# Row sums of a 32x512x1024 array on one core: one leading load of 128 consecutive rows, or two

## The chip, the cores and the metric

The kernel runs on one core of a Trainium2 chip. The metric is the device time of one execution in microseconds (us): the median of 3 runs before the change is 160.50 us (160.48 to 160.57).

## What is computed

```
x = randn(32, 512, 1024) as float32, multiplier = 0.5
out = (sum of x over its last axis * multiplier) as float32      # 32 x 512
```

That is 16,384 rows of 1024 numbers, 67.11 MB to be read, and one number per row, 0.07 MB, to be written.

## The kernel before, in words

The array is seen as 16,384 rows of 4 KB, and the 128 partitions take 128 rows each. The rows are cut in three parts:

- **The head** (L112): the first 128 rows, one row for each partition, in one load of 512 KB. ACT sums and scales each row (`act_row`, L90) into one column of the tile `column`, which DVE has cleared (L113). DVE then transposes `column` into `row` in blocks of 32x32 (L117), so that the 128 results lie in four partitions, 32 in each, and leave in a store of four runs (L188).
- **The middle** (L123 to L154): partition p takes 111 consecutive rows, so the partitions stand 111 rows apart in memory. They come in seven blocks: one of 15 rows per partition and six of 16 (`sizes`, L43), in three buffers. DVE sums a block in one instruction (`reduce_sum`, L136) into `sums` and scales it into `res` (L142). Only in the seventh block are eight of the 16 rows summed by ACT (L153).
- **The last block** (L156 to L212): 16 consecutive rows per partition, in pieces. p0 is ten rows, p1 four, p2 one row and 384 numbers of the next, e0 352 numbers, e1 the last 288. ACT and DVE share their rows; DVE uses `dve_sum` (L99), and its last instruction adds up the parts of row 15 (L210).

All loads and stores are issued by SP, in the order of the program text, into one hardware queue. A load waits on SP only if it needs a buffer that DVE frees (`free`, on `dve_done`) or is to come behind a landing (`behind`). The loads that wait for nothing, the head and the first three blocks, are moved to the program's entry by a hook (`start_loads_at_entry`, L223), ahead of SP's first drain, so that they start before the other engines do.

Around the change SP's order at the end is: loads p0, p1, p2, e0, e1 (L163 to L182); a wait for the seventh block's scaled sums (L183); the **early store** of the middle's results (L184), which waits for ACT too; the head's store (L188); and the **last store** of the last block's results (L214), which waits for the last sums. SP then waits for the early and the head's store, drains, and waits for the last one (L218 to L221).

Of the kernel before, what the change touches and what calls it, by code (L numbers as in the profile page):

```python
# [9 lines left out]
def kernel(  # L10
# [13 lines left out]
    nc = tc.nc  # L24
# [4 lines left out]
    P = nc.NUM_PARTITIONS  # L29
# [3 lines left out]
    x_flat = x.flatten_outer_dims()  # L33
    N, D = x_flat.shape
    rows = N // P
    out_flat = out.rearrange("b s -> (b s)")
    mul = float(multiplier)

    B = 16
    n_blocks = rows // B  # L40
    assert N == P * rows and rows == n_blocks * B
    Q = 32
    sizes = [B - 1] + [B] * (n_blocks - 2)  # L43
    own = 1 + sum(sizes)
    x_rows = x_flat[P : P * own, :].rearrange("(p c) d -> p c d", p=P)
    x_last = x_flat[P * own : N, :].rearrange("(p c) d -> p c d", p=P)
    out_head = out_flat[0:P].rearrange("(q c) -> q c", c=Q)
    out_rows = out_flat[P : P * own].rearrange("(p c) -> p c", p=P)
    out_last = out_flat[P * own : N].rearrange("(p c) -> p c", p=P)

    def sbuf(name, *shape):
        return ctx.enter_context(nc.sbuf_tensor(name, list(shape), fp32)).ap()
# [2 lines left out]
    buf = [sbuf(f"xb{i}", P, B, D) for i in range(bufs)]  # L55
    sums = sbuf("sums", P, rows)
    res = sbuf("res", P, rows)
    head = sbuf("head", P, 1, D)
    column = sbuf("column", P, Q)
    row = sbuf("row", P, Q)  # L60
    cuts = [384, 736, D]
# [3 lines left out]
    def sem(name):  # L65
        return nc.alloc_semaphore(name=name)
# [5 lines left out]
    def marks(i, engine):  # L72

        s = dve_done if engine == "dve" else act_done
        i.then_inc(s, 1)
        counts[engine] += 1
        return counts[engine]

    def load(name, dst, src, free=None, behind=None):

        landed = sem(name)
        i = nc.sync.dma_start(out=dst, in_=src)  # L82
        if free is not None:
            i.wait_op(dve_done, free, "sem-ge")
        if behind is not None:
            i.wait_op(behind, 16, "sem-ge")
        i.then_inc(landed, 16)
        return landed

    def act_row(t, r, dst):  # L90
        return nc.scalar.activation(  # L91
            out=t[:, r, :],
            in_=t[:, r, :],
            func=mybir.ActivationFunctionType.Copy,
            scale=mul,
            accum_out=dst,
        )
# [11 lines left out]
            accum_out=dst,  # L109
        )  # L110

    landed_head = load("landed_head", head[:, 0, :], x_flat[0:P, :])  # L112
    cleared = marks(nc.vector.memset(column, 0.0), "dve")  # L113
    nc.scalar.wait_ge(landed_head, 16)
    nc.scalar.wait_ge(dve_done, cleared)
    summed = marks(act_row(head, 0, column[:, 0:1]), "act")
    turned = nc.vector.transpose(out=row, in_=column)  # L117
    turned.wait_op(act_done, summed, "sem-ge")
    marks(turned, "dve")
# [1 line left out]
    freed = []  # L121
    blocks = []
    for b, n in enumerate(sizes):  # L123
        c0 = 1 + sum(sizes[:b])
        t = buf[b % bufs][:, 0:n, :]
        landed = load(
            f"landed{b}",
            t,
            x_rows[:, c0 - 1 : c0 - 1 + n, :],
            freed[b - bufs] if b >= bufs else None,  # L130
        )
        blocks.append(landed)
        h = n if b < n_blocks - 2 else n // 2
        nc.vector.wait_ge(landed, 16)
        done = marks(
            nc.vector.reduce_sum(  # L136
                out=sums[:, c0 : c0 + h], in_=t[:, 0:h, :], axis=mybir.AxisListType.X
            ),
            "dve",
        )  # L140
        freed.append(done)
        scaled = nc.vector.tensor_single_scalar(  # L142
            out=res[:, c0 : c0 + h],
            in_=sums[:, c0 : c0 + h],
            scalar=mul,
            op=mybir.AluOpType.mult,
        )
        scaled.wait_op(dve_done, done, "sem-ge")
        early_dve = marks(scaled, "dve")
        if h < n:  # L150
            nc.scalar.wait_ge(landed, 16)
            for r in range(h, n):
                i = act_row(t, r, res[:, c0 + r : c0 + r + 1])  # L153
            early_act = marks(i, "act")  # L154

    c0 = own  # L156
# [23 lines left out]
            )  # L180
        )
    ]  # L182
    nc.sync.wait_ge(dve_done, early_dve)  # L183
    early = nc.sync.dma_start(out=out_rows, in_=res[:, 1:own])  # L184
    early.wait_op(act_done, early_act, "sem-ge")
    early_stored = sem("early_stored")
    early.then_inc(early_stored, 16)
    first = nc.sync.dma_start(out=out_head, in_=row[0:P:Q, :])  # L188
    first_stored = sem("first_stored")
    first.then_inc(first_stored, 16)  # L190

    summed_up = sem("summed_up")
    on_act = {1, 4, 7, 9, 13, 14}
# [22 lines left out]
    stored = sem("stored")  # L216
    store.then_inc(stored, 16)
    nc.sync.wait_ge(early_stored, 16)  # L218
    nc.sync.wait_ge(first_stored, 16)
    nc.sync.drain()  # L220
    nc.sync.wait_ge(stored, 16)  # L221

# [62 lines left out]
```

## Time and profile before

| what | value |
|---|---|
| median of 3 runs | 160.50 us (160.48 to 160.57) |
| the profiled execution: its own time | 160.47 us |
| its span | 159.2 us |
| DVE busy | 119.1 us, 75% |
| ACT busy | 17.4 us, 11% |
| DMA packets | 2168, 67.18 MB, mean 422 GB/s over the span |
| chain that ended last | DMA 74%, DVE 24% |
| SP's longest wait behind the stores | 9.7 us, until DVE's last sum |

The span runs from the first recorded instruction, SP's issue of the head, to the end of the last store; the execution's own time is 1.27 us longer. The DMA row of the page's second part is the mean busy share of 16 DMA engines in tenths, and a packet is booked where it is recorded, so that a slice with few and the next with many packets belong together. L136 is a line of the kernel. In a timeline, each row gives the start and the duration in microseconds, the engine, the line, the operation, its tiles and shapes, and in brackets how long the engine had been idle and what ended that. What SP waited for gives, behind the colon, the microseconds in all, the number of waits and the longest.

### The profile page before, as it was taken

The page shows a single profiled execution, that of the slowest core. Times are in us where ns is not written, and L with a number is a line of the kernel's source. Part 1 is how long each engine was busy: PE and PEld are TensorE (multiplying, and loading weights), DVE is VectorE, ACT ScalarE, POOL GpSimd, SP SyncE. Part 2 cuts the span into 40 slices and gives each one's busy share as a digit, 9 for nine tenths or more (in the row PEclk, how much of TensorE's full clock was granted, in tenths as well). Part 3 has the DMA queues.
Part 4 walks back from the last instruction along what each step waited for, and adds up shares of the span by engine and source line. Part 5 has one row for each costly group of instructions (what it writes and reads, how often), then busy time and mean ns, then how long its engine had stood idle before and what let it go on. Part 6 is the DMA issues. An engine that isn't in the chain of part 4 may idle for free.

```text
span 159.2 us, 131 instructions
## 1 busy us (share of the span) xinstructions
DVE 119.1 (75%) x40; ACT 17.4 (11%) x31; POOL 0.2 (0%) x4
## 2 busy tenths in 40 slices
DVE  0000059995799968999599995999959999598376
ACT  2300000000000000000000000000000000397384
POOL 0000000000000000000000000000000000000000
DMA  9997996996997999969969969969989799798994
GB/s 379 494 401 340 494 527 264 527 527 264 527 461 329 527 395 395 527 280 511 527 264 527 527 264 527 494 296 527 445 346 527 346 445 527 329 453 371 420 401 151
DMA packets 2168, 67.18 MB, mean 422 GB/s; under 512 B 504, under 2 KB 760, under 8 KB 1016
## 3 DMA queue, kind: packets, MB, share of 16 engines
q1 hardware_dynamic: 2168, 67.18, 98.0%
HBM read 67.11 MB, written 0.07 MB: 422 GB/s over the span
## 4 chain that ended last, share of the span: by engine, by line
DMA 74%; DVE 24%; another core or an unknown queue 1%; SPq 1%; issue 0%
DMA xb<-in_x_dram 74%; DVE sums L136 22%; DVE xb L101 1%; SPq L82 1%; DVE end L101 0%; DVE res L142 0%; DVE res L101 0%
## 5 line engine op out<-in xcount | busy, mean ns | idle before, releaser
L136 DVE TENSOR_REDUCE sums<-xb 128x16 f32<-128x16384 f32 (+2 forms) x7 | 110.9, 15849 | 28.4 <-DMA xb<-in_x_dram 28.4
L91 ACT ACTIVATE xb<-xb 128x1024 f32<-128x1024 f32 x14 | 14.6, 1045 | 137.1 <-DMA xb<-in_x_dram 137.1
L101 DVE CUSTOM_DVE_ANT_0 xb<-xb 128x512 f32<-128x512 f32 (+1 forms) x10 | 5.9, 652 | 4.4 <-DMA xb<-in_x_dram 4.4
L91 ACT ACTIVATION_READ_ACCUMULATOR xb<-xb 128x1 f32 x14 | 2.6, 187 | 0.0
L113 DVE MEMSET column<- 128x32 f32 x1 | 0.1, 85 | 3.0 <-PEq L26 3.0
L117 DVE STREAM_TRANSPOSE row<-column 128x32 f32<-128x32 f32 x1 | 0.2, 212 | 2.6 <-ACT head L91 2.6
L91 ACT ACT_TABLE_LOAD x1 | 1.3, 1283 | 3.1 <-DVE column L113 3.1
L142 DVE TENSOR_SCALAR res<-sums 128x16 f32<-128x16 f32 (+2 forms) x7 | 1.2, 174 | 0.2
L91 ACT ACTIVATE head<-head 128x1024 f32<-128x1024 f32 x1 | 1.1, 1056 | 0.0
L101 DVE DVE_READ_ACCUMULATOR2_ANT res<- 128x1 f32 x10 | 0.8, 80 | 0.0
L101 DVE CUSTOM_DVE_ANT_0 end<-end 128x176 f32<-128x176 f32 (+1 forms) x2 | 0.7, 326 | 0.0
L91 ACT ACTIVATION_READ_ACCUMULATOR head<-head 128x1 f32 x1 | 0.2, 186 | 0.0
L101 DVE DVE_READ_ACCUMULATOR2_ANT end<- 128x1 f32 x2 | 0.2, 82 | 0.0
L266 POOL MEMSET const-bfloat16-1.0<- 128x1 bf16 x1 | 0.1, 101 | 0.0
L266 POOL MEMSET const-uint8-127<- 128x1 uint8 x1 | 0.1, 101 | 0.0
L266 POOL MEMSET const-float32-0.0<- 128x1 f32 x1 | 0.1, 98 | 0.2 <-issue 0.2
L266 POOL MEMSET const-float32-1.0<- 128x1 f32 x1 | 0.1, 98 | 0.0
## 6 DMA issues: line engine op xcount, KB each, us to landing
xb<-in_x_dram SPq DMA_DIRECT2D x1, 7680.0 KB, 21.2
xb<-in_x_dram SPq DMA_DIRECT2D x1, 5120.0 KB, 33.6
xb<-in_x_dram SPq DMA_DIRECT2D x1, 2048.0 KB, 36.4
xb<-in_x_dram SPq DMA_DIRECT2D x1, 704.0 KB, 20.8
head<-in_x_dram SPq DMA_DIRECT2D x1, 512.0 KB, 3.3
end<-in_x_dram SPq DMA_DIRECT2D x1, 176.0 KB, 19.2
end<-in_x_dram SPq DMA_DIRECT2D x1, 144.0 KB, 10.8
xb<-in_x_dram SPq DMA_DIRECT2D x6, 40.8
```

The lines of the kernel that those rows point to most:

```text
L82: i = nc.sync.dma_start(out=dst, in_=src)
L91: return nc.scalar.activation(out=t[:, r, :], in_=t[:, r, :], func=mybir.ActivationFunctionType.Copy, scale=mul, accum_out=dst,)
L101: return nc.vector.tensor_tensor_reduce(out=row[:, 0:mid], in0=row[:, 0:mid], in1=row[:, mid:], scale=scale, scalar=0.0, op0=ADD, op1=ADD, ...
L113: cleared = marks(nc.vector.memset(column, 0.0), "dve")
L117: turned = nc.vector.transpose(out=row, in_=column)
L136: nc.vector.reduce_sum(out=sums[:, c0 : c0 + h], in_=t[:, 0:h, :], axis=mybir.AxisListType.X),
L142: scaled = nc.vector.tensor_single_scalar(out=res[:, c0 : c0 + h], in_=sums[:, c0 : c0 + h], scalar=mul, op=mybir.AluOpType.mult,)
L266: nc = _bacc.Bacc("TRN2", target_bir_lowering=False, num_devices=1)
```

## The change

The head becomes two loads of 128 consecutive rows (`H = 2`), 512 KB each. Both are summed by ACT, into columns 0 and 1, and the transpose waits for the second. The middle has 110 rows per partition, in one block of 14 and six of 16. The last block is as before. The results of the two heads lie in partitions 0, 32, 64, 96 and 1, 33, 65, 97 of `row` and leave in two stores; these are now issued before the early store and before SP's wait for the scaled sums, right behind e1. The second head is one of the loads moved to the entry. Cut to what runs differently:

```diff
-    sizes = [B - 1] + [B] * (n_blocks - 2)
-    own = 1 + sum(sizes)
-    x_rows = x_flat[P : P * own, :].rearrange("(p c) d -> p c d", p=P)
+    H = 2
+    sizes = [B - H] + [B] * (n_blocks - 2)
+    own = H + sum(sizes)
+    x_rows = x_flat[P * H : P * own, :].rearrange("(p c) d -> p c d", p=P)
...
-    out_head = out_flat[0:P].rearrange("(q c) -> q c", c=Q)
-    out_rows = out_flat[P : P * own].rearrange("(p c) -> p c", p=P)
+    out_head = out_flat[0 : P * H].rearrange("(h q c) -> h q c", h=H, c=Q)
+    out_rows = out_flat[P * H : P * own].rearrange("(p c) -> p c", p=P)
...
-    head = sbuf("head", P, 1, D)
+    head = sbuf("head", P, H, D)
...
-    landed_head = load("landed_head", head[:, 0, :], x_flat[0:P, :])
+    landed_head = [
+        load(f"landed_h{h}", head[:, h, :], x_flat[h * P : (h + 1) * P, :]) for h in range(H)
+    ]
     cleared = marks(nc.vector.memset(column, 0.0), "dve")
-    nc.scalar.wait_ge(landed_head, 16)
     nc.scalar.wait_ge(dve_done, cleared)
-    summed = marks(act_row(head, 0, column[:, 0:1]), "act")
+    for h in range(H):
+        nc.scalar.wait_ge(landed_head[h], 16)
+        summed = act_row(head, h, column[:, h : h + 1])
+    summed = marks(summed, "act")
...
+    first_stored = sem("first_stored")
+    for h in range(H):
+        first = nc.sync.dma_start(out=out_head[h], in_=row[h:P:Q, :])
+        first.then_inc(first_stored, 16)
     nc.sync.wait_ge(dve_done, early_dve)
-    early = nc.sync.dma_start(out=out_rows, in_=res[:, 1:own])
+    early = nc.sync.dma_start(out=out_rows, in_=res[:, H:own])
     early.wait_op(act_done, early_act, "sem-ge")
     early_stored = sem("early_stored")
     early.then_inc(early_stored, 16)
-    first = nc.sync.dma_start(out=out_head, in_=row[0:P:Q, :])
-    first_stored = sem("first_stored")
-    first.then_inc(first_stored, 16)
...
-    nc.sync.wait_ge(first_stored, 16)
+    nc.sync.wait_ge(first_stored, 16 * H)
```

More of the change, by code (lines that the diff above doesn't have):

```diff
@@ L123 @@
     for b, n in enumerate(sizes):
-        c0 = 1 + sum(sizes[:b])
+        c0 = H + sum(sizes[:b])
         t = buf[b % bufs][:, 0:n, :]
@@ L128 @@
             t,
-            x_rows[:, c0 - 1 : c0 - 1 + n, :],
+            x_rows[:, c0 - H : c0 - H + n, :],
             freed[b - bufs] if b >= bufs else None,
```

## The prediction

> **What bounds the kernel now.** I read the chain that ended last first, then the slices and the queue, then the timeline for landing times, then what SP waited for. From the chain in order of time:
>
> ```profile
> 0.91 40.05 DMA xb<-in_x_dram
> ...
> 77.61 40.77 DMA xb<-in_x_dram
> 118.38 0.02 issue
> 118.39 36.35 DMA xb<-in_x_dram
> 154.75 0.02 issue
> 154.77 0.69 DVE xb L101
> ...
> 157.36 0.31 DVE end L101
> 157.67 0.01 DVE res L101
> ```
>
> Loads carry the chain, and its last DMA piece ends at 154.75 us. That is the landing of p1 (rows 10 to 13 of the last block, issued at 118.4). From there to 157.68 DVE works without a gap: the last two pieces, e0 and e1, are there when it reaches them. Then the last store is issued (0.34 us) and lands 1.4 us after its issue. The page's slices and queue say why the loads take that long:
>
> ```profile
> DMA  9997996996997999969969969969989799798994
> ...
> q1 hardware_dynamic: 2168, 67.18, 98.0%
> ```
>
> The 16 DMA engines work for 98.0% of the span; the digits of 6 and 7 stand beside slices of 527 GB/s and are packets booked where they end. In the timeline of DVE, each bracket shows that DVE waited for a load, so each start is a landing:
>
> ```profile
> 21.62 16.15 DVE L136 TENSOR_REDUCE sums<-xb 128x15 f32<-128x15360 f32 x1 [15.82 <-DMA xb<-in_x_dram]
> ...
> 40.98 17.22 DVE L136 TENSOR_REDUCE sums<-xb 128x16 f32<-128x16384 f32 x1 [3.00 <-DMA xb<-in_x_dram]
> ...
> 137.75 8.69 DVE L136 TENSOR_REDUCE sums<-xb 128x8 f32<-128x8192 f32 x1 [1.93 <-DMA xb<-in_x_dram]
> ...
> 149.88 0.69 DVE L101 CUSTOM_DVE_ANT_0 xb<-xb 128x512 f32<-128x512 f32 x1 [3.23 <-DMA xb<-in_x_dram]
> ...
> 154.77 0.69 DVE L101 CUSTOM_DVE_ANT_0 xb<-xb 128x512 f32<-128x512 f32 x1 [1.13 <-DMA xb<-in_x_dram]
> ```
>
> From 40.98 to 137.75 five blocks of 8,388,608 bytes land: 19.354 us each, 433.4 GB/s. From block 0 to block 1 it is 19.36 us, the same rate. So the queue never ran dry, from the first block on, and the end is the start of the stream, plus 67.11 MB at 433.4 GB/s, plus what each load adds, plus a tail of DVE and store. DVE is busy 75%, waits about 1.9 us for every block, and sets no landing.
>
> **The change, part by part.** The profiled execution took 160.47 us, of which 159.2 are the span, so 1.27 lie around it; I leave those 1.27 as they are. The median of the runs is 160.50, 0.03 above; I add that at the end.
>
> *One load more, of 128 rows.* The bytes stay: 512 KB move from block 0 (15 rows per partition, now 14) into a second head. Block 0 keeps its 128 packets (one for each partition), so 128 packets of 4 KB and 16 for the semaphore are added to the 2168, nine for each DMA engine. What does a load cost beyond its bytes? The landings of the last block tell, at 433.4 GB/s: p0, 5,242,880 bytes, should take 12.10 us and took 12.13 (149.88 - 137.75), 0.03 more. p1, 2,097,152 bytes, should take 4.84 and took 4.89, 0.05 more. p2, 720,896 bytes in packets of 5.5 KB, should take 1.66; ACT, idle until then, starts on it at 156.50, so it took 1.73, 0.07 more. The upper end is the head itself: it landed 3.3 us after its issue at 0, and block 0, 7,864,320 bytes or 18.15 us later, landed at 21.62, which leaves 0.17. The lower end: none of the five large blocks shows a cost apart from its rate, so 0 is possible. I take p2's **+0.07 us**, since its packets are nearest in size to 4 KB, and keep 0 and 0.17. It falls on the path in full: every later landing, p1's too, stands behind it in the stream.
>
> *The start.* The first load is the same one, issued at 0.00. Each load issue at the entry takes SP about 0.44 us (0.39 to 0.43 plus a gap of 0.05), so block 0's issue moves from 0.44 to about 0.88. Data flow from about 1.06 us (the first DMA slices show them there, 1.06 after the issue); the first head's 0.52 MB keep the engines until about 1.06 + 1.21 = 2.3 and the second's until 3.5, while block 0's first bytes can flow at 0.88 + 1.06 = 1.9. No gap: cost **0**. Without that cover it would be at most the 0.44 of one issue. Blocks 1 and 2 move by 0.44 too and are needed more than 15 us later.
>
> *SP gets to the entry barrier 0.44 us later.* DVE's memset now starts at 2.95 after it, so everything behind it moves: memset about 3.4, table load 3.55, first head activation 4.85.
>
> *The second head's sum.* ACT does one more ACTIVATE (1.06 us) and one more accumulator read (0.19); the transpose waits for both, at about 7.0 instead of 5.59, and takes 0.21 with two filled columns as with one. Both engines are idle there: DVE until 21.62, ACT until 137.75. Cost **0**, with 14 us of cover. The head's landing at about 4.5 is no later than ACT reaches it.
>
> *Block 0 of 14 rows.* Its sum shortens from 16.15 by one row, 17.22 - 16.15 = 1.07, and frees its buffer at about 36.8 instead of 37.8. Block 3's load is then issued 1 us sooner, into a queue that holds blocks 1 and 2, the latter landing at 60.4. No engine would have idled, so the gain is **0**.
>
> *The stores.* Now SP issues e1 (146.47), the early store (146.91, 0.37 us), and the result row (147.33, 0.64 us). After: e1 first as before, then two result rows at 0.64 each, then the early store at about 148.2 instead of 146.9. What follows on SP is the wait for the last store:
>
> ```profile
> SPq L214 <- DVE res L101: 9.7, 1, 9.7
> ```
>
> So 9.7 us become about 9.0 and the last store's issue at 157.70 doesn't move. In the queue, the early store landed 10.6 us after its issue, at 157.5, behind e1 (issued 146.47, 10.8 us to landing, 157.3): stores issued behind e1 wait behind e1, and issuing them 1.3 us later changes no order among loads. What is new is that on the few engines that serve a four-partition store there stand two packets of 128 B and their semaphore writes where one stood, before the early store's packets. By the pace of the early store (eight packets and one semaphore write per engine in about 0.2 us between 157.3 and 157.5) that is some 0.04 us, on a store that SP would not miss before the last one lands at 159.1: **0**, at worst 0.04. The early store's rows go from 444 to 440 bytes: no term.
>
> *The pitch of the rows.* Every block's partitions now stand 110 rows (440 KB) apart in HBM instead of 111 (444 KB). The trace has three pitches already: one row (the head), 111 rows (433.4 GB/s) and 16 rows, 64 KB (p0: 432.2 with its 0.03, p1: 428.9 with its 0.05). The 64 KB pitch, a pure power of two, loses nothing beyond the per-load cost, so for 440 KB, 55 times 8 KB, I take **0**. The bound above is p1's 428.9 for all that is loaded at this pitch (110 rows of 512 KB, 57.7 MB): 134.5 us against 133.1, +1.4. In the other direction nothing is to be had that a trace shows. The Trainium skill, in "DMA: Bandwidth & Descriptors", section "Latency and other measured facts", says that copies with per-partition row pitches at large powers of two lose rate and that padding the pitch by 4 KiB brings it back; by that rule an odd count of 4 KB rows is the safe pitch and this change gives it up. Against it stands p0 at a 64 KB pitch; no run here shows 440 KB.
>
> *Sum:* 160.47 + 0.07 = 160.54; on the median's scale **160.57 us**.
>
> **Rivals.** A measurement of this kernel can tell about 0.2%, 0.32 us, from no change; so "faster" is below 160.18 and "slower" above 160.82.
>
> *A, the forecast:* the extra load costs 0 to 0.17, 160.50 to 160.67. For it: four loads whose cost is read off, and a queue that is full throughout. Chance 0.64; within 0.2%.
>
> *B, the extra cost of a small first load is paid once:* the 0.17 between head and block 0 are then the time in which the engines change from the head to the first large block, and with 1 MB ahead it is hidden instead of doubled. 160.50 - 0.17 = 160.33. For it: that excess is the largest of the four. Against: block 0's first bytes could already flow at 0.44 + 1.06 = 1.5 us, 0.8 before the head's end. Chance 0.13; within 0.2%.
>
> *C, slower, the pitch:* a 440 KB pitch makes concurrent reads of the 16 engines collide in HBM. Its place is the seven blocks, its price 57.7 MB at the lower rate: each GB/s lost costs 133.1/433.4 = 0.31 us, so from about 1 GB/s on it decides. At p1's 428.9 it is 160.57 + 1.4 = 162.0; a middling loss of 2 GB/s gives 161.2. For it: the rows leave no spare rate, and the pitch gains a factor of two. Against: 64 KB does no harm. Chance 0.12.
>
> *D, the moved stores:* the two four-partition stores take more in the queue than a packet each and push the early store past the last one's landing: the last store is issued at 157.70 and lands at 159.1, the early one at 157.5, so 1.6 us are there to be used up first. A delay of 2 us, about one landing (1.4) plus one issue (0.64), would give 160.57 + 0.4 = 161.0. Chance 0.03.
>
> *E, faster by more than 0.2%:* the whole of p0's to p2's kind of cost and the head's 0.17 fall away and the rate rises by over 0.5 GB/s with the new pitch: 160.1. No row shows it. Chance 0.08.
>
> That gives faster 0.08, within 0.2% 0.77, slower 0.15. The range goes from 160.2 to 160.95: it takes in A, B and the small end of C, and leaves out most of E and of C's and D's larger losses. A and B alone would be 160.3 to 160.7.
>
> **What would show it.** Right: block 0 lands within 0.2 us of 21.62, DVE's block starts after it are 19.35 us apart, the blocks' sum at L136 has a form of 14 rows near 15.1 us, the early store is issued near 148.2 and lands near 157.6, the last store is issued at about 157.8. Wrong: a distance between blocks above 19.40 (C); block 0 earlier than 21.5 (B); SP's last wait on the early or the first store rather than on the last (D). My time fails if the start of the stream costs another amount than a load in its middle, since only one load in the trace stands there.

## The result and the profile after

The changed kernel took 161.40 us (median of 13 runs, 160.59 to 161.76) against 160.54 us before (13 runs, 160.43 to 160.65): a ratio of 1.0042, 95% interval 1.0025 to 1.0059. It is slower, and uneven: five of its runs lie at 160.59 to 160.84, eight at 161.33 to 161.76, while the kernel before stays within 0.22 us. The forecast was 160.57 us, in a range of 160.2 to 160.95. The profiled execution took 161.70 us, so it is one of the eight, and its loss is larger than that of the median; its span is 160.4.

The page of the changed kernel, its slices and its queue:

```profile
span 160.4 us, 135 instructions
...
DMA  8999998998999989989989979979979989799893
...
q1 hardware_dynamic: 2320, 67.18, 97.6%
```

There are 152 packets more: the 144 that were counted for the load, and eight for the second store of results (four of 128 B and four semaphore writes). No slice shows a hole. Where the time went, DVE's timeline tells, read as landings as before:

```profile
22.88 15.09 DVE L141 TENSOR_REDUCE sums<-xb 128x14 f32<-128x14336 f32 x1 [15.75 <-DMA xb<-in_x_dram]
...
42.22 17.22 DVE L141 TENSOR_REDUCE sums<-xb 128x16 f32<-128x16384 f32 x1 [4.04 <-DMA xb<-in_x_dram]
...
138.97 8.69 DVE L141 TENSOR_REDUCE sums<-xb 128x8 f32<-128x8192 f32 x1 [1.91 <-DMA xb<-in_x_dram]
```

Block 0 lands at 22.88 instead of 21.62, 1.26 us late. Blocks 1 to 6 then stand 19.34 to 19.36 us apart, where it was 19.31 to 19.38 before, and the span ends 1.23 us later (160.38 against 159.15). So the whole loss of this execution arises before block 0 has landed, and nothing later adds to it or takes from it.

Two stretches of the windows view show where. Their columns are the stretch, its length, the busy time and instructions of DVE, ACT and POOL, the granted clock, the DMA share and the GB/s, and a packet's bytes are booked in the stretch in which the packet starts. Before, then after:

```profile
2.50:3.00 0.50, 0.05 (x1) 0.00 (x0) 0.00 (x0) 1.00 4.95 2073
3.00:3.50 0.50, 0.04 (x1) 0.38 (x1) 0.00 (x0) 1.00 0.00 0
```

```profile
3.50:4.00 0.50, 0.01 (x1) 0.50 (x1) 0.00 (x0) 1.00 1.87 647
4.00:4.50 0.50, 0.00 (x0) 0.50 (x1) 0.00 (x0) 1.00 3.56 1278
4.50:5.00 0.50, 0.00 (x0) 0.49 (x2) 0.00 (x0) 1.00 0.34 115
5.00:6.00 1.00, 0.00 (x0) 1.00 (x3) 0.00 (x0) 1.00 0.15 57
```

A packet of block 0 is one partition's rows, and each of the 16 engines has eight of them. Before, all 16 first packets start in one stretch (16 x 61,440 bytes in 0.5 us are 1966 GB/s). After, one starts between 4.5 and 5.0 (57,344 bytes in 0.5 us are 115 GB/s) and one between 5.0 and 6.0 (57 GB/s over 1 us). The trace's records of single packets make it exact. They don't name the engine; an engine's first packet of block 0 is told by not starting where another large packet ends. Before, the engines end the head's packets at 2.59 to 2.92 and start block 0's at 2.59 to 2.93, fifteen right behind and one 0.11 us later. After, they end the second head's at 3.83 to 4.26, but the first packets of block 0 start at 3.95 to 5.25. Ten engines start right behind. The other six, among them the five that came first (3.83 to 3.92), stand idle until 4.11 to 5.25. The first packets are also slow, up to 3.43 us on engines that were on time and more than 3.1 us on one of those that waited, where the same size later takes 2.116. The engine that starts last sets the landing: from 5.25, one packet of 2.44 us and seven of 2.116 end at 22.50, and the last packet of block 0 ends at 22.48. The trace has a landing time for each engine too: those of block 0 are spread over 1.18 us (0.44 before), the spread stays 1.14 to 1.20 through all later blocks, and a load has landed when the last engine has.

At the end, the chain and the last wait of SP:

```profile
136.88 20.86 DMA xb<-in_x_dram
157.74 0.02 issue
157.76 1.15 ACT xb L92 x2
```

```profile
SPq L220 <- ACT xb L92: 9.2, 1, 9.2
```

p2's landing (157.74) and ACT's row now end last, by five hundredths. The stores cost nothing: SP still waits 9.2 us, against the 9.0 that were forecast.

### The profile page after: what moved, and what is told of

Same layout as the page of the kernel before. It is cut to its first block, busy times and chain, and to the rows that moved or that the text cites. A ratio compares the mean times of both kernels' runs of the same rounds, so it can differ in the third digit from the quotient of the medians.

```text
span 160.4 us, 135 instructions
## 1 busy us (share of the span) xinstructions
DVE 118.0 (74%) x40; ACT 18.5 (12%) x33; POOL 0.2 (0%) x4
## 4 chain that ended last, share of the span: by engine, by line
DMA 64%; DVE 32%; another core or an unknown queue 1%; SPq 1%; ACT 1%; issue 0%
DMA xb<-in_x_dram 64%; DVE sums L141 32%; SPq L83 1%; ACT xb L92 1%; DVE res L147 0%
## 5 line engine op out<-in xcount | busy, mean ns | idle before, releaser
L92 ACT ACTIVATE head<-head 128x1024 f32<-128x1024 f32 x2 | 2.1, 1048 | 0.0
```

What stands on the lines that cost most here:

```text
L92: return nc.scalar.activation(out=t[:, r, :], in_=t[:, r, :], func=mybir.ActivationFunctionType.Copy, scale=mul, accum_out=dst,)
```

## The experiments

Each kernel was timed beside the kernel before, on the same chip. The times are medians; the ratios are estimated from all runs and need not be the quotient of the medians. The theory to be tested first was that the pitch of 110 rows makes the first large packets collide (PITCH). Its rivals: two small loads ahead of the large one (SMALL LOADS, later split into the number of packets, PACKETS or COUNT, and the place as third load, LOADS), and the time at which the engines go over to large packets (MOMENT).

**split_111**, the kernel before with block 0 in two loads:

```diff
+        s0 = 1 if b == 0 else 0
+        if s0:
+            nc.vector.wait_ge(load("landed_s", t[:, 0:s0, :], x_rows[:, 0:s0, :]), 16)
         landed = load(
             f"landed{b}",
-            t,
-            x_rows[:, c0 - 1 : c0 - 1 + n, :],
+            t[:, s0:, :],
+            x_rows[:, c0 - 1 + s0 : c0 - 1 + n, :],
```

> The kernel before with block 0 in two loads: one row per partition, then 14; the pitch stays 111 rows and the sequence of loads at the entry has the sizes of the changed kernel (512 KB, 512 KB, 7168 KB). Three theories of the 1.26 us by which block 0 lands late in the changed kernel. PITCH (440 KB between partitions makes the first large packets collide): block 0 lands within 0.2 us of 21.62, 160.6 us. SMALL LOADS (two loads of 4 KB packets ahead of the first large block): block 0 lands at 22.4 to 22.9 in the profile, 161.0 to 161.7 us with a wide scatter. MOMENT (the engines go over to large packets at about 4 us instead of 2.6, whatever stands before): as SMALL LOADS.

161.43 us against 160.51, ratio 1.0051 (1.0038 to 1.0064): as slow as the changed kernel, with 111 rows of pitch. **second_late**, the changed kernel with the second head's load behind block 2 (its ACT row and the transpose follow it):

```diff
     landed_head = [
-        load(f"landed_h{h}", head[:, h, :], x_flat[h * P : (h + 1) * P, :]) for h in range(H)
+        load("landed_h0", head[:, 0, :], x_flat[0:P, :])
     ]
...
         blocks.append(landed)
+        if b == bufs - 1:
+            landed_head.append(load("landed_h1", head[:, 1, :], x_flat[P : 2 * P, :]))
```

> The changed kernel with the second head issued behind block 2, so that block 0 follows the first head as in the kernel before; the pitch is 110 rows. PITCH: block 0 lands 0.6 to 1.3 us later than it would (its bytes are 0.52 MB fewer than in the kernel before: 20.4 us without trouble, 21 to 21.7 with it), 161.0 to 161.7 us, wide scatter. SMALL LOADS: block 0 lands at 20.4, 160.6 us. MOMENT: 160.6 us.

160.63 us against 160.51, ratio 1.0009 (1.0000 to 1.0017), all eleven runs within 0.16 us. DVE's line for block 0 in split_111 and in second_late:

```profile
22.21 16.15 DVE L139 TENSOR_REDUCE sums<-xb 128x15 f32<-128x15360 f32 x1 [15.89 <-DMA xb<-in_x_dram]
```

```profile
20.50 15.09 DVE L140 TENSOR_REDUCE sums<-xb 128x14 f32<-128x14336 f32 x1 [16.97 <-DMA xb<-in_x_dram]
```

20.50 is where block 0 belongs with 0.52 MB fewer ahead of it (21.62 - 1.21 = 20.41). PITCH falls by both runs. The Trainium skill's rule on row pitches ("DMA: Bandwidth & Descriptors", section "Latency and other measured facts") speaks of large powers of two. 440 KB, 55 times 8 KB, is none, so the prediction asked more of that rule than it says when it called an odd count of rows the safe pitch; second_late reads all seven blocks at 440 KB without loss.

**one_head_256**, the changed kernel with both heads in one load of two rows per partition; the sums of partition p are the results 2p and 2p + 1 and are stored without the transpose:

```diff
+    x_head = x_flat[0 : P * H, :].rearrange("(p c) d -> p c d", p=P)
...
+    landed_head = load("landed_head", head, x_head)
...
+    first = nc.sync.dma_start(out=out_head, in_=res[:, 0:H])
```

> The changed kernel with both heads as one load of two consecutive rows per partition (8 KB packets, 1 MB); their sums leave in one store of 8 bytes per partition, without the transpose. The pitch of the blocks is 110 rows. PITCH: block 0 at 22.4 to 22.9, 161.0 to 161.7 us. SMALL LOADS: block 0 at about 21.6, 160.6 us. MOMENT: block 0 late, 161.0 to 161.7 us.

162.33 us against 160.51 (ratio 1.0120, 1.0098 to 1.0142), but as a test it is spoilt. Block 0 lands at 21.95, only 0.33 late (its first packets start right behind the head's, at 4.03 to 4.59), and the rest is at the end, in a store of 8 bytes per partition that I had added:

```profile
out_dram<-res SPq DMA_DIRECT2D x1, 55.0 KB, 12.6
out_dram<-res SPq DMA_DIRECT2D x1, 1.0 KB, 12.6
out_dram<-res SPq DMA_DIRECT2D x1, 8.0 KB, 2.6
```

The columns are tiles, issuing queue, count, size and us to landing: the last store (8 KB) takes 2.6 us instead of 1.4. Its own packets have ended at 159.04, but its last semaphore write arrives at 160.62, behind those of the 1 KB store (159.71) and the early store (160.35). That the 8-byte pieces hold them up is inferred from this order; no run tests it. This is what rival D of the prediction would have looked like.

**stores_only**, the kernel before with the head's store moved ahead of the early store:

> The kernel before with its head's store issued ahead of the early store, nothing else. All three theories and the prediction: no effect, 160.5 to 160.6 us. If the moved store mattered, the last store or the last wait of SP would move: over 160.8 us.

160.51 us against 160.51, ratio 1.0000 (0.9991 to 1.0008). The moved store is free.

**two_halves**, the kernel before with its head in two loads of 512 columns each:

```diff
+    halves = [
+        load(f"landed_h{h}", head[:, 0, lo : lo + 512], x_flat[0:P, lo : lo + 512])
+        for h, lo in enumerate((0, 512))
+    ]
```

> The kernel before with its head in two loads, one for each half of the 1024 columns (2 KB packets, 256 KB each); block 0 of 15 rows and the pitch of 111 rows stay. The number of packets ahead of the first large one is that of the changed kernel (16 and two semaphore writes per engine), the moment that of the kernel before (about 2.6 us). COUNT (many small packets ahead of the first large one delay it on some engines): block 0 lands at 22.2 to 22.9, 161.0 to 161.7 us. MOMENT (going over to large packets at about 4 us is what hurts): block 0 at 21.6 to 21.8, 160.6 us. PITCH has fallen.

162.62 us against 160.51, ratio 1.0113 (1.0084 to 1.0142); block 0 at 24.02:

```profile
24.02 16.15 DVE L140 TENSOR_REDUCE sums<-xb 128x15 f32<-128x15360 f32 x1 [17.44 <-DMA xb<-in_x_dram]
```

This is worse than with two full rows, and more than COUNT had named, at a moment that is harmless in the kernel before. **one_1mb**, the kernel before with block 0 in loads of 2 and 13 rows, issued first, and the head behind block 2:

> The kernel before with block 0 in two loads, two rows per partition (8 KB packets, 1 MB) and then 13, and the head's load issued behind block 2. Eight packets per engine stand ahead of the first large one, as in the kernel before, but the engines go over at about 3.8 us. COUNT: the 15 rows are there at about 20.4 (0.52 MB fewer stand ahead of them), 160.6 us, scatter below 0.2. MOMENT: 0.5 to 1.3 us later, 161.0 to 161.7 us.

160.61 us against 160.51, ratio 1.0009 (1.0001 to 1.0018), block 0 at 20.46, as COUNT had named (one run of eleven took 161.12):

```profile
20.46 16.15 DVE L140 TENSOR_REDUCE sums<-xb 128x15 f32<-128x15360 f32 x1 [16.84 <-DMA xb<-in_x_dram]
```

The engines go over to large packets at 3.9 to 4.3 us, as in the changed kernel, and each first packet starts right behind and lasts 1.97 us, its normal time. MOMENT falls by both. **three_small**, the kernel before with block 0 in loads of 1, 1 and 13 rows:

> The kernel before with block 0 in three loads of 1, 1 and 13 rows per partition: with the head three loads of 4 KB packets stand ahead of the first large one, 24 packets per engine; the engines go over at about 5.2 us; pitch 111. COUNT: block 0 at 22.2 or later, 161.0 to 162.5 us, at least as slow as with two. MOMENT: as slow as with two if what disturbs lasts from 3.3 to 5 us, 160.6 us if it is over by then.

161.51 us against 160.51, ratio 1.0059 (1.0044 to 1.0074): no worse than with two. In its trace the fourth load, the large one, starts on every engine within 0.1 us of the third's end (5.13 to 6.02); the loss is at the third load, a small one, whose landings spread over 0.86 us where the second's spread 0.48. **act_late**, the changed kernel with the head's memset, table load and sums behind block 0's sum:

> The changed kernel with ACT's table load, DVE's memset and both head sums held until block 0 is summed (about 38 us); loads and stores as in the changed kernel. If the start of ACT's and DVE's work at 3.4 us disturbs the loads: block 0 at 21.7, 160.6 us. COUNT, and MOMENT through anything else: no change against the changed kernel, 161.0 to 161.7 us with a scatter of 0.5 or more.

161.24 us against 160.51, ratio 1.0048 (1.0033 to 1.0063): ACT and DVE have no part in it.

That left the number of packets or the place as third load. **padded_head** cuts the one head into 16 packets per engine by a gap in its tile; **extra_16p** and **extra_128p** put a load of 64 KB, whose data nothing uses, between the head and block 0, in 1 or in 8 packets per engine (extra_128p has 128 for both the partitions and the numbers):

```diff
-    head = sbuf("head", P, 1, D)
+    head = sbuf("head", P, 2, D // 2 + 16)
...
```

```diff
+    extra = sbuf("extra", 16, 1024)
...
+    load("landed_extra", extra, x_flat[0:16, 0:1024])
```

> The kernel before with its head still one load, but cut in two packets of 2 KB per partition (the tile has a gap between the halves of the columns): 16 packets and one semaphore write per engine, 512 KB, ahead of block 0, which stays the second load. PACKETS (what counts is how many packets per engine stand ahead of the first large one; one load of eight is harmless, 16 are not): block 0 as late as with two half heads, 22.2 to 24 us, over 161.0 us. LOADS (what counts is that the first large load is the third to be issued, its packets being supplied to the engines one load after the other): block 0 at 21.6 to 21.8, 160.6 us.

> The kernel before with a second load behind the head whose data nothing uses: 16 rows once more, on 16 partitions, one 4 KB packet and a semaphore write per engine (64 KB, by their rate 0.15 us). Block 0 is the third load, with nine data packets per engine ahead of it. PACKETS: block 0 at about 21.8, 160.75 us, scatter as in the kernel before. LOADS: 161.0 to 161.8 us with a wide scatter.

> As the run before with 16 partitions, with the same 64 KB as 512 bytes on each of 128 partitions: block 0 is the third load, with 16 data packets and two semaphore writes per engine ahead of it. PACKETS: 161.0 to 162.5 us, block 0 from 22.2 us on. LOADS: the same as with 16 partitions. If neither count matters, 160.75 us for both.

161.00 us (ratio 1.0028, 1.0017 to 1.0038), 163.47 us (1.0178, 1.0164 to 1.0192) and 163.40 us (1.0167, 1.0147 to 1.0187), all against 160.58. One packet per engine more costs as much as eight, once it is a load of its own: PACKETS falls, LOADS stands, though the loss is larger than the 161.0 to 161.8 us that it had named. extra_16p's block 0:

```profile
24.95 16.15 DVE L138 TENSOR_REDUCE sums<-xb 128x15 f32<-128x15360 f32 x1 [18.68 <-DMA xb<-in_x_dram]
```

padded_head is slow for another reason. Its first packets of block 0 start right behind the head's on every engine (3.10 to 3.39); what is late is the start. SP's first issues, in the kernel before (one line) and in padded_head (two):

```profile
0.00 0.39 SPq L82 DMA_DIRECT2D head<-in_x_dram  x1
```

```profile
0.00 0.69 SPq L82 DMA_DIRECT2D head<-in_x_dram  x1
0.74 0.58 SPq L82 DMA_DIRECT2D xb<-in_x_dram  x1
```

Issuing 256 packets takes SP 0.69 us where 128 take 0.39, and the first packet starts at 1.47 us instead of 1.11. The run also settles whether block 0 is late only because SP issues it later: here its issue ends at 1.32 us, in the changed kernel at 1.34, and here no engine waits for it at 3.10. It is the load in between that counts. **head_late**, the kernel before with the head's load behind block 2 and so no small load in front:

> The kernel before with its head's load issued behind block 2, so that block 0 is the first load and no small packet stands ahead of it. Both theories: no harm, 160.5 to 160.7 us, scatter below 0.3; block 0 at about 20.4 (0.52 MB fewer ahead of it). If a small load ahead of the first large one is worth something, as a start before the large packets, this is slower than before by that.

161.21 us against 160.58, ratio 1.0039 (1.0026 to 1.0051). Neither theory had named a loss:

```profile
21.13 16.15 DVE L134 TENSOR_REDUCE sums<-xb 128x15 f32<-128x15360 f32 x1 [17.85 <-DMA xb<-in_x_dram]
```

Block 0 belongs at 20.41 here. The 16 first packets, now of 61,440 bytes, start at 1.02 to 1.99 us and last 2.46 to 3.30 us instead of 2.267. One small load ahead is worth 0.63 us. The engines' first packets are slow in the kernel before too, but there the 4 KB ones lose at most 0.31 us each; that this is the whole reason isn't shown.

What remained was why the third load is late (SUPPLY: it reaches the engines late in itself; BEHIND: the loads issued right behind it hinder it). **before_held**, **after_held** and **extra_16p_held** issue blocks 1 and 2 only after the last small load has landed; for the changed kernel:

```diff
             freed[b - bufs] if b >= bufs else None,
+            landed_head[1] if b == 1 else None,
```

> The kernel before with the loads of blocks 1 and 2 issued only when the head has landed (about 3.3 us) instead of right behind block 0's; both are needed from 21 us on. SUPPLY (the third load's packets reach the engines late, whatever follows): no change, 160.5 to 160.6 us. BEHIND (loads issued right behind the first large one slow the change to large packets): the first large packets lose their excess, 160.3 to 160.5 us.

> The changed kernel with the loads of blocks 1 and 2 issued only when the second head has landed (about 4.6 us). SUPPLY: as the changed kernel, 161.0 to 161.7 us, wide scatter. BEHIND: 160.5 to 160.7 us, scatter below 0.3, block 0 near 21.7.

> The kernel with the 64 KB on 16 partitions behind the head, its blocks 1 and 2 issued only when these 64 KB have landed (about 4 us). SUPPLY: 163.0 to 163.7 us as without that. BEHIND: 160.7 to 160.9 us.

160.57, 161.29 and 163.55 us against 160.54; ratios 1.0002 (0.9993 to 1.0010), 1.0041 (1.0025 to 1.0056) and 1.0184 (1.0171 to 1.0197). Nothing changes: BEHIND falls. **third_later** and **third_at_5** keep the large load third, with 4 or 2 rows per partition ahead of it in the second:

> The kernel before with block 0 in two loads of 4 and 11 rows per partition (16 KB and 44 KB packets): the large load is the third again, but 2.6 MB stand ahead of it, so that the engines come to it at about 7 us instead of 2.7 to 4. SUPPLY: late by nothing then, the 15 rows are there at 21.6 to 21.8, 160.6 us. BEHIND: the same. If the place as third load is what costs, whatever the time: 161.0 us or more.

> The kernel before with block 0 in two loads of 2 and 13 rows per partition: the large load is the third and the engines come to it at about 5.1 us, between the 3.9 of the run with 1 and 14 rows (+0.9 us) and the 7 of that with 4 and 11 rows (0). SUPPLY, with packets that are there on every engine at about 5.3 us at the latest (the last first-packets in the slow kernels start at 4.5 to 5.6): 160.55 to 160.75 us. If it is the place of the load among small ones: near 161.4 us.

third_later: 160.58 us against 160.54, ratio 1.0003 (0.9994 to 1.0012). Being third costs nothing when the engines come to it late:

```profile
21.75 16.15 DVE L142 TENSOR_REDUCE sums<-xb 128x15 f32<-128x15360 f32 x1 [15.37 <-DMA xb<-in_x_dram]
```

third_at_5: 160.74 us against 160.49, ratio 1.0013 (1.0003 to 1.0022). Its block 0 has landed at 21.66 and its first packets start right behind the second load's (5.28 to 5.61) and last 1.97 us, so the third load was in time; where its 0.25 us come from, I can't say (in the profiled execution p2's packets were slow, up to 0.54 us instead of 0.215, but one_1mb has such packets too, up to 0.48). **extra_other** reads the unused 64 KB from the last rows:

```diff
-    load("landed_extra", extra, x_flat[0:16, 0:1024])
+    load("landed_extra", extra, x_flat[N - 16 : N, 0:1024])
```

> The kernel with 64 KB on 16 partitions behind the head, these now read from the last 16 rows of the array instead of the first 16, which the head's packets read at the same moment. SUPPLY: as with the first 16 rows, 162.5 to 163.7 us. If reading the same rows twice at once made the loss: 160.75 us.

162.89 us against 160.49, ratio 1.0150 (1.0136 to 1.0163). 2.40 of the 2.89 us stay, so it isn't the rows read twice; whether the other 0.49 come from them or from the other chip is open.

The runs in one table, by the load that fell short; "needed" is when the first engine had ended the load ahead, "start" when the first packets of the large load start (us, from the packets' records; for three_small of its fourth load):

| kernel | large load is | needed from | start on the 16 engines | against before |
|---|---|---|---|---|
| before | second | 2.59 | 2.59 to 2.93 | |
| second_late | second | 2.51 | 2.52 to 3.03 | +0.12 |
| padded_head | second | 3.09 | 3.10 to 3.39 | +0.42 |
| one_1mb | second | 3.89 | 3.90 to 4.31 | +0.10 |
| two_halves | third | 2.43 | 2.49 to 5.43 | +2.11 |
| extra_16p | third | 2.78 | 2.79 to 6.21 | +2.89 |
| changed kernel | third | 3.83 | 3.95 to 5.25 | +0.86 |
| split_111 | third | 3.82 | 3.87 to 4.54 | +0.92 |
| third_at_5 | third | 5.28 | 5.28 to 5.61 | +0.25 |
| third_later | third | 7.63 | 7.64 to 8.03 | +0.04 |
| three_small | fourth | 5.13 | 5.13 to 6.02 | +1.00 |

So it is shown that a load issued third at the entry is not there for some engines when they come to it at 2.4 to 3.8 us. The loss is 2.1 to 2.9 us where they come at 2.4 to 2.8, about 0.9 us at 3.8, and from 5.3 us on no engine waits more than 0.1 us. It is no fixed time at which the third load arrives: in extra_16p one engine waits until 6.21, although in third_at_5 all have started by 5.61. And third_at_5 and third_later changed the packets of the load ahead with the time (8 and 16 KB instead of 4). three_small keeps 4 KB there, and its large load, wanted from 5.13 us, is in time, but as the fourth. Not shown is what happens between SP's issue, which ends at 1.34 us for block 0 of the changed kernel, and the engines. "Perfetto Trace Analysis" of the Trainium skill, section "DMA Instruction — HWDGE (DVE, Sync)", says that an issue is profiled until its descriptors are generated and the issuing sequencer is free again, and that the engines' work on them is not part of that. No run here sees the descriptors, so the 0.43 us of each issue tell nothing for or against it. Whether the packets are made late or the first reads are slow stays open: in the changed kernel the first packets are slow on engines that waited and on engines that did not.

No version tried beats the kernel before.

## Why the prediction was wrong

Its bound was right: the queue of loads sets the end, DVE and ACT do not, and any delay at the start goes to the end in full (1.26 us at block 0, 1.23 at the span's end).

The step that failed is *the start*, where the prediction put "No gap: cost **0**" and "Without that cover it would be at most the 0.44 of one issue." It took the 1.06 us between the first issue and the first packet as the delay of every load, and so had block 0's first bytes flowing at 0.88 + 1.06 = 1.9. Measured, they start at 3.95 to 5.25, up to 1 us after the last engine had ended the second head (4.26), and six engines stood idle. Nor does the cover hold to the figure: the first head keeps the engines until 2.59 to 2.92 in the trace of before, where 1.06 + 1.21 = 2.3 was put. One delay, read off the first load, was used for the third; and the bound of 0.44 was a move of SP's issue, not of what the engines get. The last sentence of the prediction named this weak place ("if the start of the stream costs another amount than a load in its middle"), but neither range nor chances followed from it.

- *One load more*, +0.07: held, where the load is not in the way. second_late has the load, the pitch and the stores of the change and costs 0.12 us (interval 0.00 to 0.27). The remaining 0.86 - 0.12 = 0.74 us are the place of the second head's load, ahead of block 0.
- *ACT, DVE, the transpose, block 0 of 14 rows*: nothing, as said (act_late; 15.09 us for the sum, 15.1 were named).
- *The stores*: nothing, as said (stores_only, ratio 1.0000; 9.2 us of wait left).
- *The pitch*: nothing, as said. Rival C had the sign and the wrong mechanism: its test, blocks more than 19.40 us apart, shows 19.34 to 19.36. That its middling price, 161.2, comes near the 161.40 measured is chance.
- Rival B, a head that pays its start once, is contradicted: block 0 came later, not earlier than 21.5.
- The digits of 6 and 7 in the DMA slices were said to be packets booked where they end; the windows show that they are booked where they start. No number hung on it.

## What to carry to other kernels

A queue that is full of bytes can still run dry at its start: read the first packets of the first loads, not only the mean share. One small load ahead of the first large one pays (head_late loses 0.63 us without it); in these runs a second one ahead of it cost 0.9 us or more unless it brought enough work to last until about 5 us, and behind the large loads the same 512 KB cost 0.1 us. A delay measured on the first transfer of a queue is no delay for the third.

## What the runs showed of the hardware

- In the changed kernel the 16 engines keep what they lost. A spread of 1.18 us at block 0's landing was still 1.2 us at p2's, 135 us later; all of them run at the same pace (2.418 us for 65,536 bytes), and none catches up.
- 64 KB that nothing uses cost 2.9 us at the entry, nearly twenty times the 0.15 us of their bytes, although they are one packet per engine.
- An engine's first packets are slow: of the head's, up to 0.47 us in the kernel before for the 0.159 of a later one; of head_late's large ones, up to 3.30 for 2.267.
- SP's issue takes longer with more packets, 0.69 us for 256 of 2 KB against 0.39 for 128 of 4 KB, and the first packet starts 0.36 us later. Below that it hardly falls: extra_16p's 16 packets took 0.42 us as the second issue, where the 128 of block 0 took 0.43.
- With a store of 8-byte pieces ahead of it, the last store landed 2.6 us after its issue instead of 1.4.
